# A streaming-encoder block in Strassen products: a group's own product inside each common product, two value products by turns from shared blocks, and P4's first step ahead of P3

## The chip, the cores and the metric

One core of a Trainium2 chip runs the whole block in one launch. The metric is the device time of one execution in microseconds; a difference of 0.2% is 4.3 us here. The engines are TensorE (PE, matmuls; PEld is its weight loads), VectorE (DVE), ScalarE (ACT), GpSimd (POOL) and SyncE (SP, which issues every DMA). The program holds for each engine a list of instructions in a fixed order, with waits on the other engines in it.

## The reference

One layer on x of 1024 tokens by 1024 channels, all in fp32 (D_FF is 2816, four heads of 256, chunks of 64):

```python
h = x + 0.5 * swiglu_ffn(rmsnorm(x, norm_ffn1), ffn1_w_in, ffn1_w_out)
u = rmsnorm(h, norm_mix)
q, k, v, g_ret, p, gates = jnp.split(u @ w_in, split_points, axis=-1)
q, k = rotary(q), rotary(k) * 256 ** -0.5
ret = retention(q, k, v)                  # chunkwise, per-head decay
ret = ret * lax.rsqrt(jnp.mean(ret * ret, -1) + eps) * jax.nn.silu(g_ret)
pool_out = multiscale_pool(p, pool_w, pool_scale)
gate = jax.nn.sigmoid(gates + gate_bias)
h = h + (gate[0] * (ret @ w_ret_up) + gate[1] * (pool_out @ w_pool_up)) @ w_out
h = h + 0.5 * swiglu_ffn(rmsnorm(h, norm_ffn2), ffn2_w_in, ffn2_w_out)
return rmsnorm(h, norm_final)
```

where `swiglu_ffn(x)` is `(silu(gate) * up) @ w_out` with gate and up the two halves of `x @ w_in`.

## The kernel before, in words

**Numbers and products.** Each fp32 operand is split into a high part (ACT copies it to fp32r, L158) and a low part (DVE subtracts, L159; the scaled form is L162 and L163). A product of two operands is three matmuls (`mm3`, L178 to L180): high by high, high by low, low by high. A wide step of a product is 12 matmuls of 128x512 on one PSUM bank or on four.

**Strassen groups.** The big products are Strassen-Winograd products of 2x2 blocks. `strassen` makes one group (two row tiles of output) out of seven products, by their index in a group: 0 is L11 by R11, 1 is S2 by T2, 2 is S1 by T1, 3 is S3 by T3, 4 is L12 by R21 (P2), 5 is S4 by R22 (P3), 6 is L22 by T4. Each is a pair (prep, body): prep combines and splits the weights on DVE and ACT, body issues the matmuls and the reads of the bank.

**Commons.** In a pair of groups A and B the two P2s have the same right operand, and the two P3s too. `common(nx, A, B, n)` makes both at once by a second Strassen level, with matmuls of 128x256, in three steps: `one` (18 matmuls), `two` (12) and `three` (12). In `two` the bank called x gets its second product and DVE reads it (the first `tt` after it, L575). In `three` six matmuls go to B's bank first, and the other six add to the bank x again, which they may do only after that read. The weights of `two` called s34 are used in `three` again.

**What sets the order.** `Flow.run` walks through the steps of all stages. It issues the prep of a step four steps (`LOOK`) ahead of its body, and after a body some waiting pieces of elementwise work (`flow.add`). The tile scheduler then orders each engine's list out of this code order and the pools. The pools that matter: six PSUM banks and two sum banks, five tiles for split weights (`wt`), four `raw` and four `tl` tiles for loads, eight `c2` half tiles.

**Stages in order of time** (from the trace): the first `ffn_in` (names `a_`) to about 425 us; the first `ffn_out` (names `b`) to 633, with P1 and P6 by turns, P2 and P7 by turns, then P5 (to 573), P3 (to 604), P4; `values` (names `v`) to 710; the projections (names such as `q1`, `t4`: `pairs`) to 1160; retention and pooling to 1395; merge and output product to 1545; the second `ffn_in` (`c_`) to 1985; the second `ffn_out` (`d`) to the end. `pairs_of_both` orders both `ffn_in`. There the first pairs have only P3 in common, the others both: P2's common stands ahead of the pair's product 3 and P3's common ahead of product 6, but in one pair (`k == some`) the two commons follow each other after the other products. In `pairs` the seven last pairs have both, after the other products, with 6 of A and of B between them.

**First `ffn_out`.** P1, P2, P5 and P3 add into banks "a", P6, P7 and P4 into banks "b" (four each, all eight of PSUM). P5 starts the banks "a" anew, and after its last step four DVE operations (`done`, L947, tile `bd`) read them. P3 starts them anew again after that. P3's inputs are loaded two steps at a time (`both`), and the last five or six of its preps split P4's right operand ahead of need (`ahead`).

**Values.** `values` is one Strassen product with four steps (k) to each of the seven products. After L11 come S2 and S1 by turns, then four steps of S4 (banks `vS`), four of S3 (banks `vL`), then L12 and L22. S4's prep loads L21, L22, L11 and L12 of its k as two raw tiles; S3's prep loads L11 and L21 of its k once more.

Of the kernel before, what the change touches and what calls it, by code (L numbers as in the profile page):

```python
# [90 lines left out]
def block_kernel(ctx: ExitStack, tc, x, x_tok, vecs, f1_in, f1_out, w_in, w_v, pool_w, w_ret, w_pool, w_o,  # L91
# [498 lines left out]


    BY_SUM = (0, 3, 1, 4, 2, 6, 5)

    def pairs(nx, groups, some, tags, last):

        groups = list(groups)
        for n in range(0, len(groups), 2):
            both = n >= 2 * some
            A, B = (g((2, 3) if both else (3,)) for g in groups[n : n + 2])
            yield A[0]  # L600
            yield then(B[0], last) if n == len(groups) - 2 else B[0]
            if not both:
                yield A[4]
                yield then(B[4], nx.blocks("R21", tags, True)) if n == 2 * some - 2 else B[4]
            yield from (A[3], A[1], B[3], B[1], A[2], B[2])
            yield from common(nx, A, B, 2 if both else 3)
            yield A[6]
            yield B[6]
            if both:
                yield from common(nx, A, B, 3)  # L610

# [9 lines left out]
    def pairs_of_both(nx, groups, first, some):  # L621
# [13 lines left out]
        for k, n in enumerate(range(n, len(groups), 2)):  # L635
# [3 lines left out]
            if k < some:  # L639
                yield A[4]  # L640
                yield then(B[4], nx.blocks("R21", [tl_] * 3, True)) if k == some - 1 else B[4]
            elif k > some:
                yield from common(nx, A, B, 2)

            yield from (A[3], A[1], B[3], B[1], A[2], B[2])
            if k != some:
                yield from common(nx, A, B, 3)
                yield A[6]
                yield B[6]
            else:  # L650
                yield from common(nx, A, B, 2)
                yield A[6]
                yield B[6]
                yield from common(nx, A, B, 3)

# [160 lines left out]
    def ffn_out(nx, ops, ready, w, res, name, sink, end, last=None):  # L816
# [26 lines left out]
        def both(key, k, src):  # L843

            if k % 2 == 0:
                t[key] = (tl if key[0] != "L" else raw)(f"{name}{key}{k}")
                n = min(2, FH - k)
                for z in range(n):
                    load(half(t[key], z), src(k + z))
            return half(t[key], k % 2)  # L850

# [65 lines left out]
        def step(n, f, k, where, start, after):  # L917
            o = {}

            def prep():  # L920
# [3 lines left out]
                if n == "p3" and not last and k >= FH // 2:  # L924
                    z = k - FH // 2
                    ahead[z] = operand(t4s(z), f"{name}p4m{z}")
# [82 lines left out]
        for k in range(FH):  # L1009
            yield step("p5", p5, k, "a", True, after5)  # L1010
        for k in range(FH):
            yield step("p3", p3, k, "a", False, after3)
        if not last:
            for k in range(FH):
                yield step("p4", p4, k, "b", False, after4)
# [217 lines left out]
    def values():  # L1233
# [10 lines left out]
        def block(n, k):  # L1244

            if n in ("L11", "L12", "L22"):
# [3 lines left out]
                return two[n][k % 2]  # L1250
            if n == "S1":

                return two.pop(("S1", k))
            if n == "S3":
                L11, L21 = fetch(f"v{n}{k}", (k, 0), (k, 1))
                tt(L11, L11, L21, SUB)
                return L11
            L21, L22 = fetch(f"v{n}a{k}", (k, 1), (k + 4, 1))
            L11, L12 = fetch(f"v{n}b{k}", (k, 0), *([(k + 4, 0)] if n == "S4" else []))
            tt(L22, L21, L22, ADD)  # L1260
            two["S1", k] = L22
            tt(L21, L22, L11, SUB)
            if n == "S2":
                return L21
            tt(L12, L12, L21, SUB)
            return L12
# [64 lines left out]
        for p in zip(product("S2", "T2", "a", False, after6), product("S1", "T1", "b", True, after5)):  # L1331
            yield from p
        yield from product("S4", "R22", "b", False, result(0, 1, lambda i: old("h", i)))
        yield from product("S3", "T3", "a", False, result(1, 1, lambda i: old("f", i)))
        yield from product("L12", "R21", "b", True, result(0, 0, lambda i: p1s.pop(i)))
# [593 lines left out]
```

## Time and profile before

| what | value |
|---|---|
| three runs | 2149.54, 2150.57, 2151.09 us (median 2150.57) |
| profiled execution: its own time | 2152.64 us |
| profiled execution: span | 2150.9 us |
| granted TensorE clock | 1.00 |
| ACT busy | 1104.0 us (51%), 2074 instructions |
| DMA | 320.95 MB, mean 149 GB/s |

The profile page gives each engine's busy time, the chain of work that ended last, and groups of instructions. A matmul's busy time there (389 ns for 128x512) is longer than the distance from one start to the next, since matmuls overlap in the array; so a busy PE still hides pauses. They are read from the timeline, whose rows are: start, duration, engine, line, operation, output tile and input tiles, sizes, and in brackets an idle time with what ended it. In views of windows each engine has its busy time with its count of instructions. In the view of a tile or line the three durations are least, median and most, in ns.

### The profile page before, as it was taken

How to read it: one execution, taken by the hardware profiler on the slowest of the kernel's cores; microseconds unless marked ns; L12 is line 12 of the kernel's file. 1: busy time of each engine (PE TensorE's matmuls, PEld its weight loads, DVE VectorE, ACT ScalarE, POOL GpSimd, SP SyncE). 2: the span in 40 equal slices, each digit the busy share in tenths (PEclk: the TensorE clock that was granted, in tenths of full speed). 3: DMA queues.
4: the chain of work that ended last, by engine and by line, in shares of the span. 5: the costliest groups of instructions: out<-in, count | busy, mean ns of one | idle time of the engine just before them, and what ended most of it. 6: DMA issues, size and time to landing. Idle time of an engine off the chain costs nothing.

```text
span 2150.9 us, 30140 instructions
## 1 busy us (share of the span) xinstructions
PE 2137.0 (99%) x10830; PEld 1814.4 (84%) x10830; DVE 1878.4 (87%) x3352; ACT 1104.0 (51%) x2074; POOL 0.2 (0%) x4
## 2 busy tenths in 40 slices
PE   9999999999999999999999999999999999999998
PEld 7888888888888888888888898888888888888887
DVE  8798888997987799999999876899988888899796
ACT  8544444454653544454447753446644544455454
POOL 0000000000000000000000000000000000000000
PEclk9999999999999999999999999999999999999999
DMA  7232423585537333333337567624133242358642
GB/s 255 77 133 74 135 86 128 180 286 185 175 118 250 108 109 119 107 129 107 119 107 245 179 215 255 225 92 162 64 100 121 74 137 84 128 181 294 196 130 100
DMA packets 120134, 320.95 MB, mean 149 GB/s; under 512 B 13232, under 2 KB 17456, under 8 KB 119984
## 3 DMA queue, kind: packets, MB, share of 16 engines
q1 hardware_dynamic: 119408, 317.98, 44.0%
q8 instruction: 85, 1.39, 0.3%
q10 hardware_dynamic: 576, 1.05, 0.1%
q14 instruction: 65, 0.53, 0.1%
HBM read 228.27 MB, written 90.70 MB: 148 GB/s over the span
## 4 chain that ended last, share of the span: by engine, by line
PE 83%; DVE 11%; DMA 2%; issue 2%; ACT 2%; SPq 0%; DVEq 0%; ACTq 0%
PE c_b L178 2%; PE c_b L180 2%; PE c_b L179 2%; PE a_b L178 2%; PE a_b L180 2%; PE a_b L179 2%; PE c_e L178 2%; PE c_e L179 2%; PE c_e L180 2%; PE a_e L179 2%; PE a_e L180 2%; PE a_e L178 2%; PE c_a L179 1%; PE c_a L178 1%; PE c_a L180 1%
## 5 line engine op out<-in xcount | busy, mean ns | idle before, releaser
L179 PE MATMUL c_b<-n3T,c_wS 128*128 128x512 f32 x176 | 68.5, 389 | 0.0
L180 PE MATMUL c_b<-n3T,c_wS 128*128 128x512 f32 x176 | 68.5, 389 | 0.0
L178 PE MATMUL c_b<-n3T,c_wS 128*128 128x512 f32 x176 | 68.2, 389 | 0.0
L178 PE MATMUL a_b<-n1T,a_wS 128*128 128x512 f32 x168 | 65.4, 389 | 0.0
L179 PE MATMUL a_b<-n1T,a_wS 128*128 128x512 f32 x168 | 65.4, 389 | 0.0
L180 PE MATMUL a_b<-n1T,a_wS 128*128 128x512 f32 x168 | 65.3, 389 | 0.0
L178 PE MATMUL a_a<-n1R,a_wL 128*128 128x512 f32 x120 | 46.7, 389 | 0.0
L179 PE MATMUL a_a<-n1R,a_wL 128*128 128x512 f32 x120 | 46.7, 389 | 0.0
L180 PE MATMUL a_a<-n1R,a_wL 128*128 128x512 f32 x120 | 46.7, 389 | 0.0
L179 PE MATMUL c_a<-n3R,c_wL 128*128 128x512 f32 x112 | 43.7, 390 | 0.0
L178 PE MATMUL c_a<-n3R,c_wL 128*128 128x512 f32 x112 | 43.6, 389 | 0.0
L180 PE MATMUL c_a<-n3R,c_wL 128*128 128x512 f32 x112 | 43.6, 389 | 0.0
L180 PEld LDWEIGHTS c_b<-n3T,c_wS 128*128 128x128 f32 x176 | 33.0, 188 | 6.9
L178 PEld LDWEIGHTS c_b<-n3T,c_wS 128*128 128x128 f32 x176 | 33.0, 188 | 6.8
L179 PEld LDWEIGHTS c_b<-n3T,c_wS 128*128 128x128 f32 x176 | 33.0, 188 | 6.8
L159 DVE TENSOR_TENSOR a_wS<-a_S,a_wS 128x512 fp32r<-128x512 f32 x45 | 30.7, 683 | 8.2 <-ACT a_wS L158 8.1
L179 PEld LDWEIGHTS a_b<-n1T,a_wS 128*128 128x128 f32 x168 | 31.5, 188 | 6.6
L178 PEld LDWEIGHTS a_b<-n1T,a_wS 128*128 128x128 f32 x168 | 31.5, 188 | 6.5
L180 PEld LDWEIGHTS a_b<-n1T,a_wS 128*128 128x128 f32 x168 | 31.5, 188 | 6.5
L159 DVE TENSOR_TENSOR c_wS<-c_S,c_wS 128x512 fp32r<-128x512 f32 x46 | 31.4, 682 | 3.7 <-ACT c_wS L158 3.6
L179 PE MATMUL c_e<-n3T,c_wL 128*128 128x512 f32 x88 | 34.4, 391 | 0.0
L178 PE MATMUL c_e<-n3T,c_wS 128*128 128x512 f32 x88 | 34.4, 391 | 0.0
(3380 smaller groups left out, 8163.2 us busy)
## 6 DMA issues: line engine op xcount, KB each, us to landing
c_ra<-in_f_in SPq DMA_DIRECT2D x22, 512.0 KB, 3.7
c_rb<-in_f_in SPq DMA_DIRECT2D x22, 512.0 KB, 4.4
a_ra<-in_f_in SPq DMA_DIRECT2D x21, 512.0 KB, 3.7
a_rb<-in_f_in SPq DMA_DIRECT2D x21, 512.0 KB, 4.5
t<-au SPq DMA_DIRECT2D x11, 512.0 KB, 4.3
b<-ag SPq DMA_DIRECT2D x11, 512.0 KB, 3.6
r<-au SPq DMA_DIRECT2D x11, 512.0 KB, 3.8
br<-r SPq DMA_DIRECT2D x11, 512.0 KB, 5.5
```

The costliest lines, as they stand in the source:

```text
L159: tt(lo, src, hi.bitcast(F32), SUB)
L178: mm(dst, w[0], m[0], start=start, stop=False, skip_group_check=True)
L179: mm(dst, w[0], m[1], start=False, stop=False, skip_group_check=True)
L180: mm(dst, w[1], m[0], start=False, stop=stop, skip_group_check=True)
```

## The change

It has three parts. `parted` puts a wide product of the pair (6 of A, 6 of B or 3 of A) between the steps `two` and `three` of each common. In the first `ffn_out` the step k=0 of P4 is run between P5 and P3; the loads of P4's two operands (`both`) are shifted by one, so that the first tile holds one half and the next ones two, and the operands split ahead are counted from there. In `values` S4 and S3 go by turns, and L11 - L21 is made from the blocks that S4's prep has loaded, so S3 loads nothing.

```diff
+    def parted(steps, between):
+        return steps[0], steps[1], between, steps[2]
...
             yield from (A[3], A[1], B[3], B[1], A[2], B[2])
-            yield from common(nx, A, B, 2 if both else 3)
-            yield A[6]
-            yield B[6]
             if both:
-                yield from common(nx, A, B, 3)
+                yield from parted(common(nx, A, B, 2), A[6])
+                yield from parted(common(nx, A, B, 3), B[6])
+            else:
+                yield from parted(common(nx, A, B, 3), A[6])
+                yield B[6]
...
-            elif k > some:
-                yield from common(nx, A, B, 2)
-            yield from (A[3], A[1], B[3], B[1], A[2], B[2])
+            if k > some:
+                yield from parted(common(nx, A, B, 2), A[3])
+            else:
+                yield A[3]
+            yield from (A[1], B[3], B[1], A[2], B[2])
             if k != some:
-                yield from common(nx, A, B, 3)
-                yield A[6]
+                yield from parted(common(nx, A, B, 3), A[6])
                 yield B[6]
             else:
-                yield from common(nx, A, B, 2)
-                yield A[6]
-                yield B[6]
-                yield from common(nx, A, B, 3)
+                yield from parted(common(nx, A, B, 2), A[6])
+                yield from parted(common(nx, A, B, 3), B[6])
...
         def both(key, k, src):
-            if k % 2 == 0:
+            at = (k + (key in ("T4", "L22") and not last)) % 2
+            if at == 0 or k == 0:
                 t[key] = (tl if key[0] != "L" else raw)(f"{name}{key}{k}")
-                n = min(2, FH - k)
-                for z in range(n):
-                    load(half(t[key], z), src(k + z))
-            return half(t[key], k % 2)
+                for z in range(at, min(2, FH - k + at)):
+                    load(half(t[key], z), src(k + z - at))
+            return half(t[key], at)
...
                 if n == "p3" and not last and k >= FH // 2:
-                    z = k - FH // 2
+                    z = k - FH // 2 + 1
...
             yield step("p5", p5, k, "a", True, after5)
+        if not last:
+            yield step("p4", p4, 0, "b", False, after4)
         for k in range(FH):
             yield step("p3", p3, k, "a", False, after3)
         if not last:
-            for k in range(FH):
+            for k in range(1, FH):
                 yield step("p4", p4, k, "b", False, after4)
...
-            if n == "S1":
-                return two.pop(("S1", k))
-            if n == "S3":
-                L11, L21 = fetch(f"v{n}{k}", (k, 0), (k, 1))
-                tt(L11, L11, L21, SUB)
-                return L11
+            if n in ("S1", "S3"):
+                return two.pop((n, k))
             L21, L22 = fetch(f"v{n}a{k}", (k, 1), (k + 4, 1))
             L11, L12 = fetch(f"v{n}b{k}", (k, 0), *([(k + 4, 0)] if n == "S4" else []))
             tt(L22, L21, L22, ADD)
-            two["S1", k] = L22
-            tt(L21, L22, L11, SUB)
             if n == "S2":
+                two["S1", k] = L22
+                tt(L21, L22, L11, SUB)
                 return L21
-            tt(L12, L12, L21, SUB)
+            tt(L22, L22, L11, SUB)
+            tt(L12, L12, L22, SUB)
+            tt(L11, L11, L21, SUB)
+            two["S3", k] = L11
             return L12
...
-        yield from product("S4", "R22", "b", False, result(0, 1, lambda i: old("h", i)))
-        yield from product("S3", "T3", "a", False, result(1, 1, lambda i: old("f", i)))
+        for p in zip(product("S4", "R22", "b", False, result(0, 1, lambda i: old("h", i))),
+                     product("S3", "T3", "a", False, result(1, 1, lambda i: old("f", i)))):
+            yield from p
```

The lists of the engines keep their lengths but for SP's, which has eight loads (256 KB each) fewer. Three places show how they move.

**PE in a common of the first `ffn_in`** (P2's common of the third pair that has both; `a_a` is the bank that `two` ends and `three` begins on, `a_x` the bank x, `a_e` the bank of product 3). Before:

```order
L179 MATMUL a_a<-n1R_365,a_ws_2722 128x256
L180 MATMUL a_a<-n1R_365,a_ws_2722 128x256
L178 MATMUL a_a<-n1R21y_1981,a_wy_2739 128x256
L179 MATMUL a_a<-n1R21y_1981,a_wy_2739 128x256
L180 MATMUL a_a<-n1R21y_1981,a_wy_2739 128x256
L178 MATMUL a_a<-n1R21y_1981,a_wy_2739 128x256
L179 MATMUL a_a<-n1R21y_1981,a_wy_2739 128x256
L180 MATMUL a_a<-n1R21y_1981,a_wy_2739 128x256
L178 MATMUL a_x_2785<-n1R21y_1951,a_ws_2722 128x256
L179 MATMUL a_x_2785<-n1R21y_1951,a_ws_2722 128x256
```

and now, at the same place:

```order
L179 MATMUL a_a<-n1R_365,a_ws_2723 128x256
L180 MATMUL a_a<-n1R_365,a_ws_2723 128x256
L178 MATMUL a_e<-n1T_574,a_wS_2743 128x512
L179 MATMUL a_e<-n1T_574,a_wS_2743 128x512
L180 MATMUL a_e<-n1T_574,a_wS_2743 128x512
L178 MATMUL a_e<-n1T_596,a_wS_2743 128x512
L179 MATMUL a_e<-n1T_596,a_wS_2743 128x512
L180 MATMUL a_e<-n1T_596,a_wS_2743 128x512
L178 MATMUL a_e<-n1T_617,a_wS_2743 128x512
L179 MATMUL a_e<-n1T_617,a_wS_2743 128x512
```

The 12 matmuls of product 3, which stood behind `three`, now stand between the last matmul of `two` and the first of `three`; the first matmul on `a_x` moves from 7 rows behind `two` to 19.

**PE and DVE at the end of P5** (`bp5a` are the banks "a", `bp6b` the banks "b"; the names `bp3m` and `bp3w` are P3's split operands, `bp4m` and `bp4w` P4's). PE before:

```order
L178 MATMUL bp5a_5225<-bp5m_5359,bp5w_5356 128x512
L179 MATMUL bp5a_5225<-bp5m_5359,bp5w_5356 128x512
L180 MATMUL bp5a_5225<-bp5m_5359,bp5w_5356 128x512
L178 MATMUL bp5a_5222<-bp3m_5380,bp3w_5377 128x512
L179 MATMUL bp5a_5222<-bp3m_5380,bp3w_5377 128x512
```

and now:

```order
L178 MATMUL bp5a_5225<-bp5m_5359,bp5w_5356 128x512
L179 MATMUL bp5a_5225<-bp5m_5359,bp5w_5356 128x512
L180 MATMUL bp5a_5225<-bp5m_5359,bp5w_5356 128x512
L178 MATMUL bp6b_4193<-bp4m_5381,bp4w_5378 128x512
L179 MATMUL bp6b_4193<-bp4m_5381,bp4w_5378 128x512
```

DVE before, up to its reads of the banks:

```order
L159 TENSOR_TENSOR bp4m_5508<-bT_5505,bp4m_5508 128x512
L159 TENSOR_TENSOR bp3m_5531<-bR_5525,bp3m_5531 128x512
L159 TENSOR_TENSOR bp4m_5534<-bT_5505,bp4m_5534 128x512
L947 TENSOR_TENSOR bd_5443<-bp5a_5222,brb 128x512
L947 TENSOR_TENSOR bd_5448<-bp5a_5223,brb 128x512
```

and now:

```order
L159 TENSOR_TENSOR bp3m_5526<-bR_5500,bp3m_5526 128x512
L159 TENSOR_TENSOR bp4m_5532<-bT_5529,bp4m_5532 128x512
L159 TENSOR_TENSOR bp3w_5438<-bs_4182,bp3w_5438 128x512
L950 TENSOR_TENSOR bd_5447<-bp5a_5222,brb 128x512
L950 TENSOR_TENSOR bd_5452<-bp5a_5223,brb 128x512
```

Twelve matmuls of P4 stand between P5 and P3 on PE. On DVE the reads stand one row later (row 848 of its list instead of 847), with a split of P3's weights ahead of them. From the first read of P3's banks to the third split of S2's weights in `values` DVE's list has 85 rows before and 83 now.

**PE in the values** (`vS` and `vL` are the banks of S4 and S3). Before, at the end of S4's first step, and now:

```order
L180 MATMUL vS_6179<-vS4w_6238,n2R_5575 128x512
L178 MATMUL vS_6176<-vS4w_6262,n2R_5578 128x512
L179 MATMUL vS_6176<-vS4w_6262,n2R_5578 128x512
L180 MATMUL vS_6176<-vS4w_6262,n2R_5578 128x512
L178 MATMUL vS_6177<-vS4w_6262,n2R_5578 128x512
```

```order
L180 MATMUL vS_6179<-vS4w_6239,n2R_5573 128x512
L178 MATMUL vL_6037<-vS3w_6254,n2T_5928 128x512
L179 MATMUL vL_6037<-vS3w_6254,n2T_5928 128x512
L180 MATMUL vL_6037<-vS3w_6254,n2T_5928 128x512
L178 MATMUL vL_6038<-vS3w_6254,n2T_5928 128x512
```

S3's first step has moved from behind S4's fourth to behind its first, and so on by turns.

## The prediction

> **What bounds the kernel now.** I read the page's busy times first.
>
> ```profile
> PE 2137.0 (99%) x10830; PEld 1814.4 (84%) x10830; DVE 1878.4 (87%) x3352; ACT 1104.0 (51%) x2074; POOL 0.2 (0%) x4
> ```
>
> PE is the bound: 99% busy. The change removes no matmul, so all it can win is pauses between matmuls, and the 99% hides those. So I read next PE's timeline from start to start, around the places that the diff touches. First the commons, four of them: from the last matmul on B's bank to the second on x, and (306) the first two on x:
>
> ```profile
> 284.44 0.28 PE L180 MATMUL a_a<-n1R21y,a_wy 128*128 128x256 f32 x1
> 284.71 0.38 PE L178 MATMUL a_x<-n1R21y,a_ws 128*128 128x256 f32 x1
> 284.94 0.28 PE L179 MATMUL a_x<-n1R21y,a_ws 128*128 128x256 f32 x1
> ...
> 306.00 0.33 PE L178 MATMUL a_x<-n1R22y,a_ws 128*128 128x256 f32 x1
> 306.16 0.28 PE L179 MATMUL a_x<-n1R22y,a_ws 128*128 128x256 f32 x1
> ...
> 321.64 0.28 PE L180 MATMUL a_a<-n1R21y,a_wy 128*128 128x256 f32 x1
> 322.18 0.39 PE L178 MATMUL a_x<-n1R21y,a_ws 128*128 128x256 f32 x1 [0.25 <-DVE ag L575]
> 322.40 0.28 PE L179 MATMUL a_x<-n1R21y,a_ws 128*128 128x256 f32 x1
> ...
> 1901.09 0.28 PE L180 MATMUL c_a<-n3R21y,c_wy 128*128 128x256 f32 x1
> ...
> 1901.43 0.28 PE L180 MATMUL c_a<-n3R21y,c_wy 128*128 128x256 f32 x1
> 1901.61 0.39 PE L178 MATMUL c_x<-n3R21y,c_ws 128*128 128x256 f32 x1
> 1901.83 0.28 PE L179 MATMUL c_x<-n3R21y,c_ws 128*128 128x256 f32 x1
> ```
>
> A narrow matmul follows the last by 0.113 us where nothing waits (1901.09 to 1901.43 is three of them). From 284.44 to 284.94 stand two, 0.50 us, so 0.27 is lost; at 322 it is 0.76 - 0.23 = 0.53; at 1901 it is 0.40 - 0.23 = 0.17. The bracket names the cause: the bank x must have been read by DVE at L575. The same core's DVE there:
>
> ```profile
> 318.16 1.22 DVE L738 TENSOR_TENSOR ag<-ag,n1rb 128x1024 f32<-128x1024 f32 x1
> ...
> 321.10 0.69 DVE L441 TENSOR_TENSOR a_S<-a_S,a_ra 128x512 f32<-128x512 f32 x1
> 321.70 0.42 DVE L575 TENSOR_TENSOR ag<-a_x,ag 128x256 f32<-128x256 f32 x1
> 322.04 0.68 DVE L159 TENSOR_TENSOR a_wS<-a_S,a_wS 128x512 fp32r<-128x512 f32 x1
> ```
>
> DVE had no pause; the read was queued behind other work and started at 321.70, when PE had already issued everything ahead of x.
>
> **Part 1: a product within each common.** It adds and removes nothing; between the read's earliest time and PE's need of it now lie 6 narrow matmuls (0.68 us) plus 12 wide ones. A wide step is 12 x 0.227 = 2.72 us (pitch from the S1 rows further down: 654.74 to 656.33 is seven matmuls). The longest delay found here is 0.53 us, and even the longest DVE operation in these rows (1.22 us) is under 2.72. So this wait goes wherever it stands. The places in the trace: four in the first ffn_in (284.71 to 396.56: 0.27, 0.53, 0.24, 0.28) and five in the second (1715.77 to 1901.61: 0.28, 0.33, 0.33, 0.36, 0.17), 2.79 us together. Beside them ten P3 commons lose some 0.05 us behind x's first matmul (306.00 to 306.16 is 0.16), and in three places of the projections about 0.12: 1.0 in all. No bracket says that these are the same wait, so the bounds are 0 and 1.0, and I take 0.5, since they stand at the same matmul of `three`.
>
> What it costs: s34's weight tile is used in `two` and `three` and so is held 2.72 us longer, and there are five such tiles. Where two commons now follow each other (seven pairs of the projections, one pair of each ffn_in) a product's weights can be split only once the product five steps earlier has let its tile go. By the steps' pitches the shortest lead falls from one wide plus one `one` (2.72 + 18 x 0.113 = 4.8 us) to a `two` plus a `one` (1.37 + 2.05 = 3.4 us). Needed are a copy on ACT and a subtraction on DVE:
>
> ```profile
> L158 ACT CAST vS3w<-vS x4: 620/620/621, 675.6 to 683.5; 128x512 fp32r<-128x512 f32 x4
> ```
>
> 0.62 + 0.68 (L159 above) = 1.3 us, and 2.5 with the 1.22 us operation ahead on DVE. That is covered by 3.4; I take nothing for it, and what it costs without cover is the third rival. The reads behind the moved products (A's evacuation) come later than before by no more than a step and free banks that, in the new order, no product needs for two steps or more.
>
> **Part 2: P4's first step.**
>
> ```profile
> 573.47 0.39 PE L180 MATMUL bp5a<-bp5m,bp5w 128*128 128x512 f32 x1
> 574.64 0.47 PE L178 MATMUL bp5a<-bp3m,bp3w 128*128 128x512 f32 x1 [0.79 <-DVE bd L947]
> 574.95 0.40 PE L179 MATMUL bp5a<-bp3m,bp3w 128*128 128x512 f32 x1
> ...
> 573.21 0.69 DVE L159 TENSOR_TENSOR bp4m<-bT,bp4m 128x512 fp32r<-128x512 f32 x1
> 573.81 2.48 DVE L947 TENSOR_TENSOR bd<-bp5a,brb 128x512 f32<-128x512 f32 x4
> ```
>
> Two pitches are 0.45 us, here they take 1.48: 1.03 us are lost, because DVE gets to `bd` only at 573.81, behind splits. With 2.72 us of P4 in between, the first read may come 1.7 us later than it does; it comes one row (0.60 us, the distance from 573.21 to 573.81) later, so the pause goes. But P3's end then lies 2.72 - 1.03 = 1.69 us later, and what hangs on it is DVE:
>
> ```profile
> 603.00:633.00 30.00, 30.00 (x134) 24.82 (x134) 29.88 (x49) 18.16 (x32) 0.00 (x0) 1.00 0.33 106
> 633.00:660.00 27.00, 27.00 (x119) 22.06 (x118) 26.67 (x44) 13.16 (x24) 0.00 (x0) 1.00 0.52 164
> ...
> 603.40 2.48 DVE L947 TENSOR_TENSOR bd<-bp5a,brb 128x512 f32<-128x512 f32 x4
> ...
> 654.74 0.39 PE L180 MATMUL vS<-vS1w,n2T 128*128 128x512 f32 x1
> ...
> 656.33 0.39 PE L178 MATMUL vL<-vS2w,n2T 128*128 128x512 f32 x1
> 656.70 0.50 PE L179 MATMUL vL<-vS2w,n2T 128*128 128x512 f32 x1
> 657.04 0.40 PE L180 MATMUL vL<-vS2w,n2T 128*128 128x512 f32 x1
> ...
> 655.97 0.68 DVE L159 TENSOR_TENSOR vS2w<-vS2a,vS2w 128x512 fp32r<-128x512 f32 x1
> ```
>
> From the first read of P3's banks at 603.40 DVE works without a gap (29.88 of 30, 26.67 of 27), and at its far end PE waits for it: 0.71 us for two pitches at 656.33, so 0.25 lost, behind the `vS2w` split that starts at 655.97. That run of DVE now starts 1.69 us later and holds two operations fewer (1.2 us), so it ends 0.5 us later. PE, which is bound there, would not keep the 1.03 but lose 0.5 against before. What is late next is that split. Bounds: -1.03 (DVE catches up by another order) and +0.5; the rows stand for the latter, which I take. The Trainium skill, page "TensorE: Matmul & The Clock Gate", section "Architectural detail: the array is 16× 32×32, not 1× 128×128", says that VectorE's queue is strict FIFO while TensorE's may draw weight loads ahead. By this rule DVE can't take the late split first, which is the +0.5; the trace agrees, since at 573.81 the `bd` reads stood behind splits that PE did not yet need. Were it not so, the term would be -1.03.
>
> **Part 3: the values.**
>
> ```profile
> 675.64 0.39 PE L178 MATMUL vS<-vS4w,n2R 128*128 128x512 f32 x1
> 676.15 0.50 PE L179 MATMUL vS<-vS4w,n2R 128*128 128x512 f32 x1
> ...
> 681.50 0.39 PE L178 MATMUL vL<-vS3w,n2T 128*128 128x512 f32 x1
> 682.26 0.50 PE L179 MATMUL vL<-vS3w,n2T 128*128 128x512 f32 x1 [0.37 <-DVE vS3w L159]
> 682.59 0.39 PE L180 MATMUL vL<-vS3w,n2T 128*128 128x512 f32 x1
> ...
> 665.00:680.00 15.00, 14.88 (x66) 12.02 (x65) 10.73 (x17) 6.32 (x11) 0.00 (x0) 1.00 0.88 286
> ```
>
> Pauses of 0.28 and 0.53, each followed by a slow second pitch (0.11 more): 1.03 us. DVE is busy only 10.73 of these 15 us while the DMA engines are at 0.88: the splits wait for loads, not for DVE. Eight loads of 256 KB go, 2.1 MB, and each k now keeps PE for two wide steps (5.44 us) on one pair of raw tiles, with six DVE operations (3.6 us). Both terms leave room, so -1.0; bounds 0 (the two raw tiles come free later, since S3's split holds them) and -1.03. L12's first product takes the banks of S4, which were read 10.9 us ahead of it and now only one wide step, 2.72 us; four reads of 0.6 fit.
>
> **A side effect.** At 913.72 PE waits for a split of t4's weights that on DVE stands behind a 1024 wide operation:
>
> ```profile
> 913.72 0.40 PE L179 MATMUL t4e<-n2T,t4wS 128*128 128x512 f32 x1
> 914.55 0.50 PE L180 MATMUL t4e<-n2T,t4wS 128*128 128x512 f32 x1 [0.43 <-DVE t4wS L159]
> 1184.16 0.38 PE L180 MATMUL s<-q,k 128*128 128x256 f32 x1 [1.20 <-DVE k L159]
> ```
>
> 0.83 - 0.23 = 0.6 lost. In the new order the split stands ahead of that operation: between 0 and -0.6; I take -0.6, since nothing else is in the row's bracket. The retention's start (1184.16, 1.2 us) is reordered too; which way it goes I can't tell, 0 with 1 us to either side.
>
> **Sum.** -2.8 - 0.5 + 0.5 - 1.0 - 0.6 = -4.4 us. The profiled execution took 2152.64 us with a span of 2150.87; the three runs have a median of 2150.57. All terms lie within the span, so I take them from the median: **2146.2 us**.
>
> **The rivals.** *P4's gain is kept* (-1.0 in place of +0.5): 2144.7. For it speaks that the scheduler has moved other DVE rows too; against it the two gapless windows. *The pauses only move*: DVE is 87% busy and often without a gap, so a PE that comes earlier waits at the next split instead; then only the values (cause: DMA) gain, 2149.5. For it speaks the 656.70 row, and every pause above but one set has DVE as its releaser; against it that DVE as a whole is idle 13% of the span, so that a delay of half a microsecond can be made good. *Adjacent commons starve for weights*: at nine places the lead is 3.4 us and a split needs 1.3; with four operations queued ahead on DVE (1.22 and three of 0.68, 3.3 us) PE lacks 1.2 us at each, -4.4 + 9 x 1.2 = +6.4, 2157.0, slower than before. It decides from the point where more than 2.1 us are queued ahead of such a split; for it speaks that DVE's rows up to 321.70 have no gap, against it that the splits of these weights stand early in DVE's new list. That the change does nothing is excluded by the moved rows.
>
> **How the numbers follow.** About 0.2%, 4.3 us, is what a measurement can tell here; faster means below 2146.3, slower above 2154.9. Forecast 0.48 (its own range 2144.7 to 2148; 0.28 of it below 2146.3, 0.20 above), P4's gain kept 0.20 (faster), pauses only move 0.22 (no change), starved weights 0.10 (slower). So faster 0.48, same 0.42, slower 0.10. The range goes down to the kept gain with the upper bound of the small pauses and 1 us from the retention (2143.2), and up to the moved pauses with a lost side effect and 1 us of the retention (2151.1); only the starved weights lie outside.
>
> **What would show it.** Right: in the commons, x's first matmul 0.113 us behind the one before; no idle between P5, P4 and P3, and a pause of about 0.7 us in S2's third step of the values; no pause in `vS4w` and `vS3w`'s products, and DMA below 0.88 there. Wrong: brackets `<-DVE` with weights (`wL`, `wS`, `ws`) ahead of the second commons, a wait of L12's first product for the reads of S4's banks, or new pauses in the retention of over 1 us.

## The result, and the profile after

The changed kernel takes 2154.91 us (median of 22 runs, 2151.15 to 2158.81) against 2151.52 of the kernel before in the same jobs (22 runs): a ratio of 1.0015 with an interval of 1.0009 to 1.0021. It is slower by some 3.4 us (1.9 to 4.5), where 4.4 us of gain were forecast; the forecast's range ended at 2151.1. The profiled execution took 2156.33 us with a span of 2154.5 us, against 2152.64 and 2150.87 before. The page's first part, the busy times of the changed kernel:

```profile
PE 2139.3 (99%) x10830; PEld 1815.4 (84%) x10830; DVE 1877.7 (87%) x3352; ACT 1097.7 (51%) x2074; POOL 0.2 (0%) x4
```

The matmuls are the same 10830, and PE is busy 2.3 us longer than before (2139.3 against 2137.0). Nothing in this line says why. As in the prediction, I went to PE's timeline and took the distance of each matmul's start from the one before, less the pitch of its shape (0.227 us for 512 columns, 0.114 for fewer); what exceeds the pitch by more than 0.03 us I call a pause, also where PE is not idle but slow. Summed by stage, in us (the kernels e1 to e12 are those of the next section):

| kernel | first ffn_in (280–470) | its P7 (470–565) | P5 to P3 (565–633) | values (633–715) | projections (715–1160) | retention (1160–1395) | second ffn_in (1690–1980) | its P7 to end (1980–) | the rest | sum |
|---|---|---|---|---|---|---|---|---|---|---|
| before | 1.54 | 0 | 1.03 | 1.38 | 1.52 | 5.10 | 1.89 | 1.24 | 7.96 | 21.66 |
| after | 0.45 | 0.91 | 0.03 | 1.37 | 1.20 | 10.04 | 0.27 | 2.71 | 7.17 | 24.15 |
| e1 projections alone | 2.02 | 0 | 0.86 | 1.44 | 1.87 | 10.59 | 2.27 | 0.98 | 7.15 | 27.18 |
| e2 all but projections | 0.11 | 2.27 | 0 | 1.02 | 1.46 | 5.12 | 0 | 2.40 | 7.01 | 19.39 |
| e3 last pair of projections old | 0 | 0 | 0 | 1.37 | 1.44 | 5.41 | 0.04 | 1.18 | 7.76 | 17.20 |
| e4 last pairs of ffn_in old too | 0.06 | 0 | 0 | 1.16 | 1.27 | 4.55 | 0.05 | 0.73 | 7.92 | 15.74 |
| e8 e4 without P4's step ahead | 0.06 | 0 | 0.29 | 0.35 | 1.53 | 4.65 | 0.06 | 0.64 | 6.58 | 14.16 |
| e9 pool's loads in own tiles | 0 | 1.38 | 0 | 0.96 | 1.06 | 6.09 | 0 | 2.50 | 7.05 | 19.04 |

Each row is one execution, and a cell scatters from one to the next also where nothing was changed. With the projections as before, retention has 4.12 to 5.64 us in e5, e6 and e7 against 5.10 and the projections 1.33 to 1.96 against 1.52; with the ffn_in as before, P7 to the end has 0.98 to 1.50 in e1, e5 and e6 against 1.24. So a difference of half a microsecond in one cell says nothing by itself.

The two rows on top tell the story. The stages that the change aimed at gained: 2.7 us in the two ffn_in, 1.0 at P5 to P3. Retention, in which no line was changed, lost 4.9 us, and behind each ffn_in stand new pauses in P7. The starts of the stages say the same: retention's first matmul comes 1.0 us earlier than before (1160.44 against 1161.47), and the stage behind retention starts 3.7 us later (1364.49 against 1360.83).

**What went as forecast.** PE's timeline of the changed kernel in the common that stood in the prediction at 321.64, and from P5 by P4 to P3:

```profile
323.75 0.28 PE L180 MATMUL a_a<-n1R21y,a_wy 128*128 128x256 f32 x1
323.86 0.28 PE L178 MATMUL a_x<-n1R21y,a_ws 128*128 128x256 f32 x1
323.98 0.28 PE L179 MATMUL a_x<-n1R21y,a_ws 128*128 128x256 f32 x1
...
573.12 0.39 PE L180 MATMUL bp5a<-bp5m,bp5w 128*128 128x512 f32 x1
573.34 0.39 PE L178 MATMUL bp6b<-bp4m,bp4w 128*128 128x512 f32 x1
...
575.84 0.39 PE L180 MATMUL bp6b<-bp4m,bp4w 128*128 128x512 f32 x1
576.06 0.42 PE L178 MATMUL bp5a<-bp3m,bp3w 128*128 128x512 f32 x1
```

The starts on `a_x` follow by 0.11 and 0.12 us, where it was 0.54 and 0.22. From P5's last matmul to P3's first are 13 pitches in 2.94 us, 0.226 each. But the third and the fourth step of S2 in the values now have a bracket each, and behind them S4 and S3 run without a pause (columns of the second view: stretch, its length, then busy time and instructions of PE, PEld, DVE, ACT and POOL, granted clock, DMA share, GB/s):

```profile
655.69 1.21 PE L178 MATMUL vL<-vS2w,n2T 128*128 128x512 f32 x4 [0.28 <-ACT vS2w L158]
...
661.96 0.50 PE L179 MATMUL vL<-vS2w,n2T 128*128 128x512 f32 x1 [0.27 <-DVE vS2w L159]
```

```profile
665.00:680.00 15.00, 15.00 (x67) 12.40 (x67) 12.33 (x20) 7.03 (x13) 0.00 (x0) 1.00 0.74 232
```

The pauses in S4 and S3 are gone and the DMA share fell from 0.88 to 0.74, as forecast. S2's pauses grew from 0.25 to 1.28 us, so that the stage as a whole stands where it was (1.38 and 1.37).

**Where the time went.** PE's timeline of the changed kernel where retention begins:

```profile
1169.31 0.39 PE L180 MATMUL px<-pl,pw 128*128 128x512 f32 x1
1171.53 0.39 PE L178 MATMUL st<-v,kd 128*128 128x256 f32 x1 [1.83 <-ACT kd L162]
...
1172.36 0.39 PE L180 MATMUL st<-v,kd 128*128 128x256 f32 x1 [0.32 <-DVE kd L163]
...
1172.81 0.48 PE L180 MATMUL st<-v,kd 128*128 128x256 f32 x1
1173.99 0.58 PE L178 MATMUL st<-v,kd 128*128 128x256 f32 x1 [0.70 <-ACT kd L162]
...
1174.59 0.41 PE L178 MATMUL ob<-v,sm 128*128 128x256 f32 x1
1174.80 0.41 PE L178 MATMUL st<-v,kd 128*128 128x256 f32 x1
```

Three pauses (1.99, 0.49 and 1.07 us, with the slow second steps behind them 4.0 in all) wait for `kd`, which ACT makes. And from 1174.59 on two matmuls of 256 columns stand 0.21 us apart, not 0.12: the clock has fallen. The windows of the changed kernel, columns as above:

```profile
1168.00:1172.00 4.00, 2.17 (x10) 1.38 (x8) 1.94 (x4) 2.04 (x5) 0.00 (x0) 1.00 0.99 368
1172.00:1174.00 2.00, 0.97 (x6) 0.65 (x5) 2.00 (x5) 2.00 (x5) 0.00 (x0) 0.70 0.78 289
1174.00:1178.00 4.00, 4.00 (x18) 4.00 (x19) 3.31 (x7) 2.95 (x6) 0.00 (x0) 0.50 0.47 149
1178.00:1180.00 2.00, 2.00 (x12) 2.00 (x12) 0.92 (x2) 1.54 (x4) 0.00 (x0) 0.59 0.64 246
1180.00:1184.00 4.00, 4.00 (x29) 3.68 (x29) 3.85 (x7) 4.00 (x9) 0.00 (x0) 1.00 0.60 145
```

From 1174 to 1178 PE is busy all 4.00 us and yet does only 18 matmuls, at a granted clock of 0.50. 25 steps up to 1179.69 are 0.10 us longer each, 2.5 us. With the 4.0 this makes 6.5 us. Two pauses that stood here before (1184.16 with 1.3 us and 1198.75 with 0.7, 2.3 with their second steps) are gone, presumably since what PE waited for there has meanwhile come. That leaves 4.2 of the 4.9 us; the rest are small pauses later in the stage, the longest 0.4 us at 1281.

Why is `kd` late? ACT's timeline, first of the changed kernel, then of the kernel before:

```profile
1165.91 1.06 ACT L1190 ACTIVATE g3A<-g3A 128x1024 f32<-128x1024 f32 x1 [0.25 <-DVE g3A L1157]
1169.96 1.14 ACT L158 CAST pl<-pl 128x512 fp32r<-128x512 f32 x2 [3.00 <-DMA pl<-p]
1171.01 0.83 ACT L162 ACTIVATE kd<-kd00b,by 128x256 fp32r<-128x256 f32 x2
```

```profile
1154.21 2.41 ACT L158 CAST pl<-pl 128x512 fp32r<-128x512 f32 x4 [1.69 <-DMA pl<-p]
...
1164.86 0.91 ACT L162 ACTIVATE kd<-kd00b,by 128x256 fp32r<-128x256 f32 x2
```

ACT stood idle for 3.00 us in front of a cast of the pool's operand `pl`, whose load had not landed, with `kd` next in its list. ACT's order of the two is not new: in both kernels, and in all of e1 to e12, eight casts of `pl` (two for each of four loads) stand ahead of the first `kd`. Before, the last four of them ran at 1154.21, ten microseconds ahead of `kd`, because their loads had landed. So what changed is the load: it is late. The issue of these two loads on SP, with the rows ahead of them, and the DVE split that lets go of a raw tile of the projections' last weights, of the changed kernel, then of the kernel before:

```profile
1156.33 0.32 SPq L137 DMA_DIRECT2D g<-g2B  x1
...
1157.21 0.96 SPq L137 DMA_DIRECT2D pl<-p  x1
...
1162.90 0.32 SPq L137 DMA_DIRECT2D g<-g3B  x1
...
1163.74 0.77 SPq L137 DMA_DIRECT2D pl<-p  x1
...
1155.62 0.68 DVE L159 TENSOR_TENSOR g3wL<-g3rb,g3wL 128x512 fp32r<-128x512 f32 x1
```

```profile
1149.77 1.58 SPq L137 DMA_DIRECT2D pl<-p  x2
...
1149.99 0.68 DVE L159 TENSOR_TENSOR g3wL<-g3rb,g3wL 128x512 fp32r<-128x512 f32 x1
```

`g3wL` are the weights of B's product 6 in the last pair. In the new order this product stands between `two` and `three` of the second common; its split moves from 1149.99 to 1155.62, and `g3rb`, one of four raw tiles, is free 5.6 us later. The pool's loads take raw tiles too; before, SP waited 1.7 us for this very split with one of them. The two loads go out at 1157.21 and 1163.74, not both within 1.6 us from 1149.77 on: some 7 and 13 us later. The tile's release by itself, at 1156.30, can account for the first at most. Both loads have also moved back in SP's list, behind the stores of `g2B` and `g3B`, which wait for ACT. The second goes out right behind such a store and a load of `k`, so what holds it is its place in SP's list. That the scheduler gave them these places because of the tile is what e9 tests.

**Behind the ffn_in.** PE of the changed kernel in the second ffn_out, then the load of weights `bL` (SP) and the DVE operation that waits for it in the first, of the changed kernel; last the same load before:

```profile
1993.56 0.39 PE L180 MATMUL dp1a<-dp2m,dp2w 128*128 128x512 f32 x1
1994.95 0.50 PE L178 MATMUL dp6b<-dp7m,dp7w 128*128 128x512 f32 x1 [1.00 <-DVE dacc L947]
```

```profile
475.39 0.81 SPq L137 DMA_DIRECT2D bL<-in_f_out  x2
...
480.03 1.35 DVE L894 TENSOR_TENSOR bs<-bL,bs 128x512 f32<-128x512 f32 x2 [1.65 <-DMA bL<-in_f_out]
...
484.92 0.68 DVE L947 TENSOR_TENSOR bacc<-bp6b,bp 128x512 f32<-128x512 f32 x1
```

```profile
471.68 0.81 SPq L137 DMA_DIRECT2D bL<-in_f_out  x2
```

P7 waits for DVE to read P6's bank (`acc`). That read stands in DVE's list behind operations on weights whose load is issued 3.7 us later than before. SP's list has changed ahead of it: the last group's stores (`t`, `b`, `r`, `m`) and P1's weight loads have changed places. But the order is not all of it. By their names, the lists of all engines are the same row by row in the changed kernel, e2, e3 and e9 up to 700 us and again from 1225 us to the end, and yet P7's pauses in the first ffn_out are 0.91, 2.27, 0 and 1.38 us there. They follow the landing of `bL`: DVE's second operation on it starts at 478.40 in e3, with no pause, and at 481.56 in e2, with the longest. Why the same lists bring it at different times the runs don't show.

### The profile page after: what moved, and what is told of

Read it like the earlier page. It is cut to its first block, busy times and chain, and to the rows that moved or that the text cites. A ratio compares the mean times of both kernels' runs of the same rounds, so it can differ in the third digit from the quotient of the medians.

```text
span 2154.5 us, 30225 instructions
## 1 busy us (share of the span) xinstructions
PE 2139.3 (99%) x10830; PEld 1815.4 (84%) x10830; DVE 1877.7 (87%) x3352; ACT 1097.7 (51%) x2074; POOL 0.2 (0%) x4
## 4 chain that ended last, share of the span: by engine, by line
PE 88%; DVE 7%; DMA 3%; issue 1%; ACT 1%; SPq 0%; DVEq 0%; ACTq 0%
PE c_b L178 2%; PE c_b L179 2%; PE c_b L180 2%; PE a_b L178 2%; PE a_b L179 2%; PE a_b L180 2%; PE c_e L178 2%; PE c_e L179 2%; PE c_e L180 2%; PE a_e L178 2%; PE a_e L179 2%; PE a_e L180 2%; PE a_a L178 1%; PE a_a L180 1%; PE a_a L179 1%; PE c_a L179 1%
## 5 line engine op out<-in xcount | busy, mean ns | idle before, releaser
L178 PE MATMUL c_e<-n3T,c_wL 128*128 128x512 f32 x88 | 34.5, 392 | 0.0
L179 PE MATMUL c_e<-n3T,c_wL 128*128 128x512 f32 x88 | 34.5, 392 | 0.0
```

The source lines that it names most:

```text
L178: mm(dst, w[0], m[0], start=start, stop=False, skip_group_check=True)
L179: mm(dst, w[0], m[1], start=False, stop=False, skip_group_check=True)
```

## The experiments

Ratios are to the kernel before in the same job, with its interval; its medians were 2151.75 (e1 to e4), 2152.09 (e5 to e8) and 2151.8 us (e9 to e12).

**e1 to e4: which part loses, and where in it.** e1 is the kernel before with the new order in `pairs` (the projections) alone; e2 is the change without it:

```diff
 e1, against before; e2 takes these lines back, against after
-            yield from common(nx, A, B, 2 if both else 3)
-            yield A[6]
-            yield B[6]
             if both:
-                yield from common(nx, A, B, 3)
+                yield from parted(common(nx, A, B, 2), A[6])
+                yield from parted(common(nx, A, B, 3), B[6])
+            else:
+                yield from parted(common(nx, A, B, 3), A[6])
+                yield B[6]
```

e3 is the change with the old order in the last pair of the projections, and e4 has it in the last pair of each ffn_in as well:

```diff
 e3 and e4, in pairs
-            if both:
+            if n == len(groups) - 2:
+                yield from (*common(nx, A, B, 2), A[6], B[6], *common(nx, A, B, 3))
+            elif both:
 e4, in pairs_of_both
+            final = n == len(groups) - 2
-            if k > some:
+            if k > some and not final:
                 yield from parted(common(nx, A, B, 2), A[3])
+            elif final:
+                yield from (*common(nx, A, B, 2), A[3])
...
-            if k != some:
+            if final:
+                yield from (*common(nx, A, B, 3), A[6], B[6])
+            elif k != some:
```

> Only the projections are changed: a product within each common there; the ffn_in stages, the first ffn_out and the values are as before. Theory A (ACT's list at the retention's start: the casts of the pool's input, which wait for a load, stand ahead of the kd activations that PE waits for): the pauses at 1160 to 1395 us rise from 5.1 to about 10 us, with a granted clock near 0.83 in the 20 us behind the projections; time +4 to +5 us against before, slower than the whole change's +3.4. Theory B (PE comes earlier everywhere and meets a saturated DVE): with only the projections' 0.4 us won, the retention stays at 5.1 and the time within 1 us of before.

> The whole change but for the projections, which are as before. Theory A: no pause of over 1.5 us at the retention's start, clock 1.00 there, pauses at 1160 to 1395 us about 5.1; the pauses in all about 19 us (24.1 with the change, less 4.9, less nothing else), time 1 to 2 us below before. Theory B: the retention's pauses stay near 10 us and the time stays 3 us above before, since PE still comes early.

> The whole change, but the last pair of the projections has its two commons as before, with both products between them. It is the smallest edit that puts the kd activations ahead of the second pair of pool casts again in ACT's list. Theory A: like all but the projections, within 1 us of that run, clock 1.00 at the retention's start. Theory B or any cause in the other six pairs: a pause of 4 us and the dip of the clock stay.

> As the run before, and in both ffn_in stages the last pair too has its commons and products in the old order. Theory C (the pauses ahead of P7 in both ffn_outs, 0.9 and 1.6 us, come from SP's list: stores of the last group's results now stand ahead of the loads of P1's weights and hold them): these pauses go, -2.2 us against the run before, and the kernel is about 3.5 us below before, about 2148. Rival (the loads are late because the DMA engines are busy, or PE is early): P7's pauses stay within 0.5 us of what they are, and the time equals the run before.

e1: 2156.85 us, 1.0024 (1.0014 to 1.0034), above the whole change's 1.0015. e2: 2151.64, 0.9996 (0.9987 to 1.0005). e3: 2149.36, 0.9990 (0.9981 to 0.9999). e4: 2147.72, 0.9983 (0.9974 to 0.9992). In e1 the waits of retention's first 30 us (what waited, for what, us in all, times, longest) are the chain found above, alone:

```profile
ACT pl L158 <- DMA pl<-p: 4.8, 2, 4.3
...
PE st L178 <- ACT kd L162: 4.0, 2, 3.1
```

In e3, with the last pair of the projections as before, these lines are absent, retention has 5.41 us of pauses in place of 10.04, and the clock is full:

```profile
1160.00:1172.00 12.00, 12.00 (x83) 11.03 (x82) 11.35 (x22) 9.72 (x19) 0.00 (x0) 1.00 0.79 291
1172.00:1180.00 8.00, 7.97 (x46) 6.58 (x44) 8.00 (x15) 6.59 (x13) 0.00 (x0) 1.00 0.80 228
```

So the last pair of the projections is the whole loss at retention. It is the loads' time that e3 restores (1147.78 and 1155.38), not an order of `kd` and the casts, as its expectation has it. e2 tells the other: without the projections' part the gains come out in the pauses (19.39 against 21.66), but P7 and what follows it lose 3.4 us more than before in that execution (2.27, and 2.40 against 1.24), and the time is no better, where 1 to 2 us below before were expected. e4 has no pause in P7 at all, but neither has e3 in the first ffn_out, with the new order; its interval overlaps e3's, so that the times alone do not part these two.

**e5 to e8: each of the other parts alone, and the best.** e5 is P4's first step alone, e6 the values alone, e7 the new order in ffn_in alone, each as in the diff of the change; e8 is e4 with P4's step back behind P3 (the loads of `both` and the operands split ahead are put back too):

```diff
 e8, against e4
-        if not last:
-            yield step("p4", p4, 0, "b", False, after4)
         for k in range(FH):
             yield step("p3", p3, k, "a", False, after3)
         if not last:
-            for k in range(1, FH):
+            for k in range(FH):
```

> Only P4's first step is moved ahead of P3. Theory (DVE is without a gap from P3's end to S2's third step of the values, so the pause moves): no pause between P5, P4 and P3 (1.03 us with the kernel before), the pauses in S2's third and fourth step of the values together 0.8 to 1.5 us instead of 0.25, time within 0.5 us of before. Rival (the 1.03 us is kept): pauses in S2 as before, time 1 us below.

> Only the values are changed: S4 and S3 by turns from the same blocks, eight loads fewer. Forecast's term: the two pauses of S4's and S3's last steps (1.03 us with their second halves) go, S2's pause of 0.25 stays; time 1 us below before. Rival (the raw tiles come free later and new pauses take their place): as many pauses at 665 to 690 us as before.

> Only the two ffn_in stages are changed. Waits for x's read: the pauses at 284 to 470 and 1690 to 1980 us fall from 3.4 to under 0.6 us together, and those at 116 to 280 and 1545 to 1690 by 0.5. SP's list (loads of P1's and P2's weights behind stores of the last group): pauses ahead of P7 of 0.5 to 2.3 us in one or both ffn_outs; time 1 to 3 us below before. Rival (the pauses ahead of P7 came from the projections or P4's loads): none ahead of P7, time 3.3 us below before.

> The run with both last pairs in the old order, and P4's first step behind P3 again. If P4's gain is taken back by DVE: the pause of 1.0 us behind P5 is back, S2's pauses fall by about as much (from 0.9 to about 0.25), time within 0.5 us of that run. If it is kept: 1 us slower than that run.

e5: 2153.36, 1.0005 (0.9996 to 1.0014), not to be told from no change. In its profile P5 to P3 falls from 1.03 to 0, and the values rise from 1.38 to 2.00, by S2's third and fourth step. e6: 2150.14, 0.9993 (0.9984 to 1.0001); the values fall from 1.38 to 0.35. e7: 2153.90, 1.0010 (1.0001 to 1.0018); the pauses of the two ffn_in fall by 2.9 us, and 1.75 come back in P7 (0.41 in the first, and 2.58 against 1.24 behind the second). The time is 1.8 us above that of before, where 1 to 3 below were expected. Its profiled execution took 2152.01 us, 1.9 less than its median, so that it does not show all of what the median lost; that part stays open. e8: 2147.63, 0.9979 (0.9970 to 0.9988), the best version of the study, 4.5 us faster than the kernel before. e8 and e4 differ by P4's step alone and are 0.1 us apart against different medians of before (ratios 0.9979 and 0.9983), so that the times can't tell what P4's step is worth. In the profiles the values fall from 1.16 to 0.35 without it, as expected, but the pause behind P5 comes back with 0.29 us only, not 1.0. With the old order this pause is anything from 0.29 to 1.17 us (e1, e6, e7, e8, e10, e12), so what the step gains there depends on the execution; S2 gives back 0.6 to 1.0 us (e5; the change).

**e9: the raw tile.** If the loss at retention comes from the raw tile that is held longer, tiles of their own for the pool's second pair of loads must undo it, with the order of products as in the change:

```diff
 e9, against after
-                r = raw(f"pl{n}{i}")
+                r = sb.tile([P, S], F32, tag="mv", bufs=N_MV, name=f"pl{n}{i}") if n == 1 else raw(f"pl{n}{i}")
```

> The whole change with its order of the projections, but the two loads of the pool's second group go to tiles of their own (of the mv pool) and no longer wait for the raw tiles that the last pair's weights hold. Theory A' (raw tile held until B's product 6, three steps later than before; load late; cast waits in ACT's list; kd late; PE pauses; the clock falls): the loads are issued before 1157 us, no pause of over 1.5 us at the retention's start, clock 1.00 there, time about 2149.5, 5 us below the whole change. Rival (the projections' new order itself makes kd late, by DVE or PE): pause and dip stay, time within 1 us of the whole change.

2151.21 us, 0.9998 (0.9989 to 1.0007): 3.7 us less than the change's median, where 5 were expected. SP's, ACT's and PE's lines of e9, each from its timeline, and the window:

```profile
1146.35 0.38 SPq L137 DMA_DIRECT2D pl<-p  x1
...
1156.25 1.01 SPq L137 DMA_DIRECT2D pl<-p  x1
```

```profile
1163.99 0.47 ACT L162 ACTIVATE kd<-kd00b,by 128x256 fp32r<-128x256 f32 x1
```

```profile
1168.38 0.39 PE L180 MATMUL px<-pl,pw 128*128 128x512 f32 x1
1168.61 0.28 PE L178 MATMUL st<-v,kd 128*128 128x256 f32 x1
```

```profile
1160.00:1172.00 12.00, 12.00 (x83) 11.03 (x82) 11.24 (x23) 9.29 (x18) 0.00 (x0) 1.00 0.95 350
1172.00:1180.00 8.00, 7.71 (x48) 6.58 (x47) 7.92 (x14) 8.00 (x17) 0.00 (x0) 1.00 0.43 136
```

The two loads go out 11 and 7.5 us earlier than in the change, `kd` starts 7 us earlier, its product follows the one before in 0.23 us, and the clock stays at 1.00. Retention has 6.09 us of pauses. The edit touches nothing but these tiles (the scheduler then moves some rows near `kd` as well; on ACT, for example, `g3A` goes behind it), and in SP's list the first load now stands ahead of `v` and the second right behind the store of `g2B` and a load of `q`. So the tile is the cause, by the chain raw tile, the loads' places in SP's list, load, cast in ACT's list, `kd`, PE, clock. The pauses in P7 (1.38, and 2.50 behind the second ffn_in) stay, so they have another cause.

**e10 and e11: the stores at the end of ffn_in.** e10 is e7 with the last group's four stores on POOL's queue; e11 is the whole change with this edit and e9's:

```diff
+                store = load if k < FH - 1 else nc.gpsimd.dma_start
...
-                    load(B[k], e["n"])
+                    store(B[k], e["n"])
...
-                    load(R[k], lo)
-                    load(T[k], hi)
+                    store(R[k], lo)
+                    store(T[k], hi)
...
-                    load(T4[k], e["m"])
+                    store(T4[k], e["m"])
```

> Only the two ffn_in stages are changed, and the stores of their last group go out by GpSimd's queue, so that SP's list has P1's loads without them. Theory C (the stores wait for the last group's elementwise work and hold the loads behind them in SP's list): no pauses ahead of P7 in either ffn_out (0.4 and 1.6 us in the run with the ffn_in stages alone), P1's loads issued some 4 us earlier, time 3 to 4 us below that run and 2 us below before. Rival (the loads wait for raw tiles or the DMA engines): pauses and time as in that run.

> The whole change with both of the above: own tiles for the pool's second group, and the last group's stores by GpSimd's queue. If the two late loads are all that the change costs: pauses in all about 16 to 17 us against 21.7 before, time 4 to 5 us below before (2147.5), like the runs with the old last pairs. If the order within the commons costs something else: over 1.5 us slower than that.

e10: 2154.91, 1.0014 (1.0005 to 1.0023); e11: 2151.32, 0.9998 (0.9990 to 1.0007). Neither did what was expected: e10 is 1.0 us above e7, not 3 to 4 below, and e11 is 3.8 us above 2147.5, with 20.8 us of pauses in place of 16 to 17. So the two late loads are not all that the change costs. P7 has no pause in either, but P6, ahead of it, has one now (in e11 1.04 us in the first ffn_out and 1.45 in the second). Two waits of e10 between 420 and 450 us:

```profile
DVE bs L872 <- DMA bra<-in_f_out: 3.1, 1, 3.1
PE bp6b L179 <- DVE bp6m L159: 1.2, 1, 1.2
```

The pause moved to an earlier load (`bra`, P1's weights), for which DVE waits 3.1 us, and nothing was won. So the stores on SP's list are not the whole of it, and e10 doesn't tell whether P7 is cured or only reached later. Against the order alone as the cause speaks e3, which has the new order in ffn_in's last pair, the same lists as the change there, and pauses of 0 and 0.24 us in P7; for it, that e4 and e8, with the old one, have none. What decides the size stays open.

**e12: the clock by itself.** On e8, eight copies of the bank on ACT ahead of `kd` (their output is used by nothing) delay `kd`. The lists of all engines are those of e8 up to there; behind it the scheduler also moves some rows on PE and DVE and one load of `v` on SP:

```diff
 e12, against e8
+        idle = c2(f"{name}idle") if name == "kd00" else None
...
+            for z in range(8 if name == "kd00" and jj == 0 else 0):
+                with soon():
+                    copy(idle, b)
```

> The fastest version so far (last pairs in the old order, P4's first step behind P3) with eight copies of a bank on ACT ahead of kd, some 4.5 us, which make PE pause at the retention's start and change nothing else; their result is not used. If the clock falls because PE pauses: a pause of 3 to 4.5 us, and a granted clock of 0.5 for 3 us or more behind it, so that the time rises by the pause and half of that stretch. If the clock's fall had another cause (the DMA load, chance): clock 1.00 and the time rises by the pause alone.

2153.19 us in its one run, and a span of 2151.4 us against e8's 2144.2. PE's row and the windows of e12:

```profile
1171.60 0.58 PE L178 MATMUL st<-v,kd 128*128 128x256 f32 x1 [3.31 <-ACT kd L162]
```

```profile
1168.00:1172.00 4.00, 0.69 (x4) 0.40 (x3) 1.17 (x4) 3.69 (x8) 0.00 (x0) 0.91 0.97 343
1172.00:1174.00 2.00, 1.92 (x8) 1.53 (x8) 1.93 (x5) 2.00 (x5) 0.00 (x0) 0.50 0.99 395
1174.00:1176.00 2.00, 2.00 (x9) 1.81 (x8) 2.00 (x5) 1.98 (x5) 0.00 (x0) 0.50 0.19 76
1176.00:1178.00 2.00, 2.00 (x12) 2.00 (x11) 0.63 (x2) 0.43 (x1) 0.00 (x0) 0.50 0.00 0
1178.00:1180.00 2.00, 2.00 (x18) 2.00 (x18) 1.81 (x3) 2.00 (x5) 0.00 (x0) 0.96 0.00 0
```

A late `kd`, made so on ACT and by no load, makes the dip too: a pause of 3.5 us, then 6 us at half the clock, also where the DMA engines do nothing (share 0.00), so that it isn't contention for them. Retention's pauses rise from 4.65 to 9.92 us; the other 2 us of the span lie in other stages of the two executions.

## Why the prediction was wrong

- *The step that failed* is the last sentence of the side effects: "The retention's start (1184.16, 1.2 us) is reordered too; which way it goes I can't tell, 0 with 1 us to either side." It measured +4.9 us. I took the existing wait at 1184.16 as the size of what could happen there, and looked at the order of the splits. What happened is a wait of another kind at 1171.53: the moved product holds a raw tile 5.6 us longer, the next user of that pool of four is a load of the next stage, and ACT's list has the cast of that load ahead of what PE needs, as it had before, when the load came in time. e3 (order back) and e9 (tile freed) each take it away. The clock, at 1.00 in all of the prediction's rows, added 2.5 us that no bound there held.
- The prediction did see that tiles are held longer ("s34's weight tile is used in `two` and `three` and so is held 2.72 us longer"), and priced it by the next split of the same stage. For the moved product 6 and its raw tile this was not done.
- *The commons*: -2.8 and -0.5 forecast. The two ffn_in fell by 2.71 in the changed kernel and by 3.3 to 3.4 in e2, e3 and e4, and the small pauses of the P3 commons ahead of them (116 to 280 and 1545 to 1690 us) by 0.6. The mechanism and the size were right. Not priced: that the new order of the last pair shifts loads of the next stage, by 3.7 us for `bL`. This is an omission of the same kind as at retention. Behind the two ffn_in 2.4 us were lost in the profiled execution (0.91, and 2.71 against 1.24), but since e3 has the same lists and none of the first loss, the order alone doesn't set it.
- *P4's first step*: +0.5 forecast, as 1.03 won and 1.5 lost at S2. The pause of 1.03 went, and the loss is at S2, as said, behind the ACT and DVE rows of `vS2w`. The loss measured 0.62 (e5), 0.81 (e4 against e8) and 1.03 (the change), and in e8, without the step, the pause behind P5 is 0.29 only. So the sum lies between -0.4 (e5) and +0.5 (e4 against e8): the mechanism was right, the size is within the scatter of these executions, and "P4's gain is kept" didn't come true.
- *The values*: -1.0 forecast; e6 and the window of 665 to 680 us confirm it, and the DMA share fell below 0.88.
- *t4's side effect*: -0.6 forecast. The pause at 914.55 has gone, but smaller ones of 0.5 together stand at 916. The projections as a whole fell by 0.32, which is less than their scatter from execution to execution.
- *The rivals*: weights that starve at adjacent commons would have given 2157.0, which lies near what was measured, but the place is wrong: the brackets on weights that it asked for aren't there, and e4 has all but three pairs of the new order and is faster. Of the signs that were named as disproof, "new pauses in the retention of over 1 us" is the one that came.
- *The range* counts one thing twice: its top of 2151.1 adds a lost side effect to "the pauses only move", whose 2149.5 holds no side effect any more. By its own terms it ends near 2150.5.

With the old order in the last pairs of the projections and of both ffn_in the sum holds: e4's pauses are 5.9 us below those of before and its ratio of 0.9983 stands for 3.7 us (1.7 to 5.6), where 4.4 were forecast for all places.

## What to carry to other kernels

When a product is moved within a stage, ask at the stage's last pass which tile it holds longer and whose load is next in that pool, even if that load belongs to another stage; then follow that load to the first in-order list that waits for it, and see what stands behind it there. A reorder that is good in a loop's middle may be bad in its last pass, and the last pass can then be left as it was: here this turned +3.4 us into -4.0. A pause of some microseconds is not to be priced by its length alone where the clock can fall with it.

## What the runs showed of the hardware

The granted clock fell to half after two pauses that were each shorter than 2.3 us. In the changed kernel PE started a wide matmul at 1169.31, the next, narrow, at 1171.53, and five more narrow ones up to 1172.81, with pauses of 1.99 and 0.49 us. In windows of half a microsecond the clock is 1.00 up to 1172.5, 0.82 from there to 1173.0 and 0.50 from 1173.0 on. So the third pause, which ended at 1173.99, fell into the slow stretch and is not what began it; from 1180 on the clock is back at 1.00. The Trainium skill, page "TensorE: Matmul & The Clock Gate", section "What's actually happening", gives half the clock for after an idle window of some 3.4 us; section "HAM oscillation — how this bites in real kernels" states it as no gap over that length. e12's single gap of 3.5 us agrees with it. The changed kernel has no such gap, so by this run two shorter gaps close together do it too. A single pause of 1.3 us (1184.16 before) had no dip behind it. The price was 2.5 us there on top of 4.0 us of waiting.
